# Small loads moved to another queue and the entry of the second block put in another order, in a two-block transformer kernel

## The chip, the cores and the metric

The kernel runs on one core of one Trainium2 chip. The metric is the device time of one execution in microseconds; three timed runs of the kernel before gave a median of 1160.46 us (1156.91 to 1160.65). The core's engines are named as in the profile: PE (TensorE, with PEld for its weight loads), DVE (VectorE), ACT (ScalarE), POOL (GpSimd) and SP (SyncE, which here only issues transfers).

## The reference, cut to what matters

The reference is a network of two blocks on 256 tokens of width 1024, in float32. The first block has two adaptive-norm layers (differential attention with rotary embedding and a context of 256 tokens, then a multi-scale pooling layer), each with a gated feed-forward network; the modulation vectors come from a matrix product with the condition. The second block takes the first one's output:

```
def second_block(x, norm1_g, norm2_g, w_in, qk_norm_g, ...):
    h = _rms(x, norm1_g[layer])
    (a_q, a_k, a_v, i_q, i_k, i_w, b_q, b_kv, b_g, c_qkv, mix_g) = _split_last(h @ w_in[layer], IN_SIZES)
    a_q = _rms(a_q.reshape(bsz, seq, A_HEADS, HEAD_DIM), qk[0])
    a_k = _rms(a_k, qk[1])
    y_a = _dsa_attention(a_q, a_k, a_v, i_q..., i_k, i_w, rel_a) @ w_branch_a[layer]
    ...                     # y_b: compressed, selected and windowed keys; y_c: dilated attention
    x = x + (g[:, :, 0] * y_a + g[:, :, 1] * y_b + g[:, :, 2] * y_c) @ w_out[layer]
    ...                     # second norm and feed-forward network
```

Branch A scores all keys with small index heads (`i_q`, `i_k`, `i_w`), keeps the 64 best keys for each query, and runs softmax attention over them.

## The kernel before, in words

**Matrix products.** Tokens stand in two tiles of 128 (`t` = 0, 1). Each float32 operand is split into a high part (`hi`, a cast on ACT, line 70) and a low part (`lo`, a subtraction on DVE, line 71), and `mm3` (lines 77 to 80) makes three matmuls of each product. Weights come in units of up to 1 MB: `raw_load` (line 54) takes one of four `raw` buffers and starts the load on SP; `wsplit` writes the two parts into a slot, chosen in rotation by `seq["w"]`: slots 0 and 1 are the two buffers of the tag `w`, the others lie in the pools of `extras`.

**Order.** A planner orders each engine's instructions from the order of the program and their dependences. `with behind(i)` orders what is issued inside it behind instruction `i` on that instruction's own engine, without a wait on other engines. A queue runs its instructions strictly in its order, so a waiting instruction holds what stands behind it.

**The first projection.** The weights of the first head group of the first attention are loaded in four quarters by `load_quarter` (keys, queries, values: lines 526 and 498), and the products follow quarter by quarter; `rest(q)` makes the values' and the context keys' part. Behind it seven small loads are issued by ACT (lines 642 to 658): five pieces of `prow` (norm gains and offsets as rows, which line 648 transposes into columns `pcol`), the rotary tables `rope` and the four vectors `lamr` for the differential weight. `rope_T` (lines 676 to 691) rotates keys and queries with four steps on DVE into `r12` and transposes them on PE (line 690).

**The end of the first block.** `o3` is the last output product, with 11 weight units, of which the last three are held and finished per tile and half: `o3.finish(t, n)`. `Norm.pre` adds the residual, `layer_norm` and `rms` normalise the tile (ACT squares with a sum, a square root, a reciprocal, a scaling at line 303), and `to_hT` transposes the scaled tile (line 320) and splits it into `hT` (ACT line 333, DVE lines 336 and 337).

**The entry of the second block.** `KZ`, a zero-padded key buffer, is cleared by POOL (line 936), which then loads `small` (masks, line 946) and `pr2` (positions and gains of queries and keys, lines 951 to 954); `pr2` is transposed at line 956 into `pc2`. `WA` are the bias tables of branch A, loaded by SP. `project(512, 452)` makes keys, values and index heads (`PA`), `project(0, 512, ...)` the queries (`PQ`). For each tile, index queries and keys are copied, transposed (line 1158) and split by `put_q` and `put_k`; `normed_dup_T` norms the keys (line 1042, then the transposes of line 1003). The index scores (line 1169) feed the search for the 64 best (lines 1178 and 1179, on DVE, as a filler of low rank). `gates(0)` makes four gate units with weights as the stationary operand.

`keep_busy(n)` issues `n` matmuls of 128 by 128 ones into a bank that nobody reads.

Of the kernel before, what the change touches and what calls it, by code (L numbers as in the profile page):

```python
# [31 lines left out]
def tile_net(ctx: ExitStack, tc: tile.TileContext, I: dict, out: bass.AP):  # L32
# [49 lines left out]
    def kview(w):  # L82
        return w.rearrange("(k p) n -> p k n", p=128)
# [264 lines left out]
    class Out:  # L348
# [7 lines left out]
        def part(self, u, wh, wl, t, n):  # L356
            mh, ml = self.mov
            tk = slice(t * 128, (t + 1) * 128)
            for k in range(2):
                kk = 2 * u + k  # L360
                mm3(self.P[t][n], mh[:, kk, tk], ml[:, kk, tk], wh[:, k, HALF[n]], wl[:, k, HALF[n]], kk == 0,
                    kk == 2 * self.nu - 1)

        def unit(self, u):
# [105 lines left out]
    with tc.tile_pool(name="at", bufs=1, side="right", reuse_waits="tile") as at:  # L470
# [48 lines left out]
        def load_quarter(q):  # L519

            raws = [raw_load(wv0[:, :, j0 * 128:(j0 + 2) * 128], 8, 256) for j0 in (8 + 2 * q, 2 * q)]
            load_x("x", q)
            rw = wp.tile([128, 2048], F32, tag="raw", name="raw", bufs=4)
            rw = rw[:, :1536].rearrange("p (w k c) -> p w k c", w=3, k=2)
            for i, kind in enumerate((1, 0, 2)):
                sp.dma_start(rw[:, i], wq[:, 2 * q:2 * q + 2, kind * 1024:kind * 1024 + 256])
                if i == 1:
                    load_x("ctx", q)
            return raws, rw
# [41 lines left out]
        class Chunk:  # L571
# [19 lines left out]
            def products(self, ks, lat=True, con=True):  # L591
                wh, wl = self.w
                kw = dict(skip_group_check=True)
                for t in range(2) if lat else ():
                    tk = slice(t * 128, (t + 1) * 128)
                    for k in ks:
                        mm3(self.PL[:, t, :], hT[0][:, k, tk], hT[1][:, k, tk], wh[:, k, :], wl[:, k, :],
                            k == 0 and t == 0, k == 7, **kw)
                if self.kind and con:
                    if self.PC is None:  # L600
                        self.PC = bank().rearrange("p (t c) -> p t c", t=2)
                    for t in range(2):
                        tk = slice(t * 128, (t + 1) * 128)
                        for k in ks:
                            if self.kind == 1:
                                mm3(self.PC[:, t, :], wh[:, k, tk], wl[:, k, tk], hc[0][:, k, :], hc[1][:, k, :],
                                    k == 0 and t == 0, k == 7, **kw)
                            else:
                                mm3(self.PC[:, t, :], hc[0][:, k, tk], hc[1][:, k, tk], wh[:, k, :], wl[:, k, :],
                                    k == 0 and t == 0, k == 7, **kw)  # L610

        ALLK = range(8)
        ck, cq, cv = (Chunk(kind, 0) for kind in (1, 0, 2))
# [2 lines left out]
        def rest(q):  # L616
            ks = range(2 * q, 2 * q + 2)
            cv.products(ks, con=False)
            ck.products(ks, lat=False)

        for q in range(4):
            with behind(*((first_dma.ins,) if not q else ())):
                raws, rw = load_quarter(q)
            mod_quarter(q, raws)
# [11 lines left out]
        oT = [oc.tile([128, 2048], F32R, tag="oT" + i, name="oT", bufs=1).rearrange("p (k c) -> p k c", k=8)  # L636
              for i in ("hi", "lo")]

        with behind(seq["mod"]):
            prow = cp.tile([128, 128], F32, name="prow")  # L640
            gp.memset(prow, 0.0)
            se.dma_start(prow[32:64], I["ln_g"].rearrange("l w (k c) -> (l w k) c", c=128))
            se.dma_start(prow[64:96], I["ln_b"].rearrange("l w (k c) -> (l w k) c", c=128))
            se.dma_start(prow[96:104], rows128(I["norm1_g_2"][0]))
            se.dma_start(prow[104:112], rows128(I["norm2_g_2"][0]))
            se.dma_start(prow[112:113], I["attn_subln_g"])
# [8 lines left out]
            rope = at.tile([128, 2, 2, 2, 64], F32, name="rope")  # L655
            se.dma_start(rope, I["k_rope"].rearrange("(t p) v w c -> p t v w c", p=128))
            lamr = at.tile([128, 256], F32, tag="aT", name="lamr", bufs=5)
            se.dma_start(lamr, I["attn_lambda"].rearrange("a b c -> a (b c)").to_broadcast([128, 256]))
# [231 lines left out]
    with tc.tile_pool(name="hid", bufs=1, side="right", reuse_waits="tile") as hidp:  # L890
# [32 lines left out]
    blk1.close()  # L923
    wi = kview(I["w_in_2"][0])
# [3 lines left out]
    seq["w"] = 2  # L928
    extras.append(ctx.enter_context(tc.tile_pool(name="wz", bufs=1, side="right", reuse_waits="tile")))
    with tc.tile_pool(name="b2", bufs=1, reuse_waits="tile") as b2:  # L930

        KZ = b2.tile([128, 6, 2, 2, 256], F32R, name="KZ")
        for half in range(2):
            gp.memset(KZ[(1 - half) * 64:(2 - half) * 64, :, :, half, :].bitcast(F32), 0.0)

        def vtile():
            return b2.tile([128, 1536], F32, tag="vv", name="vv", bufs=1)
# [4 lines left out]

        small = b2.tile([128, 554], F32, name="small")
        gp.dma_start(small, I["k_small"])
        cmask, eo, bmask = small[:, 0:256], small[:, 256:384], small[:, 384:392]
        nmask = small[:, 392:426].rearrange("p (t n) -> p t n", t=2)
        sel32 = small[0:32, 426:554]
        pr2 = b2.tile([128, 128], F32, tag="t512", name="pr2", bufs=3)  # L950
        gp.memset(pr2, 0.0)
        gp.dma_start(pr2[0:32], I["nsa_cmp_pos_2"][0].rearrange("s (l a) d -> (s l) (a d)", a=2))
        for dup in range(2):
            gp.dma_start(pr2[32:38, dup * 64:(dup + 1) * 64], I["qk_norm_g_2"][0])
        b = tbank()
        pe.transpose(b[:, :128], pr2, ident)
        pc2 = b2.tile([128, 41], F32, name="pc2")
        ve.tensor_copy(pc2[:, 0:38], b[:, 0:38])
        ve.tensor_mul(pc2[:, 38:41], b[:, 32:38:2], pc2[:, 33:38:2])
# [45 lines left out]

        def put(hi, lo, src, scale):

            se.activation(hi, src, AF.Copy, scale=scale)
            ve.scalar_tensor_tensor(lo, src, scale, hi.bitcast(F32), op0=ALU.mult, op1=ALU.subtract)

        def put_k(src, t, d0, scale=1.0):

            n, tk = src.shape[1], slice(t * 128, (t + 1) * 128)
            for half in range(2):
                p = slice(half * 64, (half + 1) * 64)
                put(KZ[p, d0:d0 + n, 0, half, tk], KZ[p, d0:d0 + n, 1, half, tk], src[p],
                    scale if isinstance(scale, float) else scale[p])
# [87 lines left out]
        def gates(br):  # L1105
            g = b2.tile([128, 8, 256], F32, tag="gate", name="gate", bufs=1)
            for u in range(4):
                wh, wl = wunit(wi[:, :, 4572 + br * 1024 + u * 256:4572 + br * 1024 + (u + 1) * 256], 8, 256)
# [78 lines left out]
        for t in range(2):  # L1187
# [270 lines left out]
```

## Time and profile before

| | us |
|---|---|
| median of three timed runs | 1160.46 (1156.91 to 1160.65) |
| the profiled execution, whole | 1157.81 |
| its span, first to last instruction | 1156.0 |
| PE busy | 1129.1 |
| DVE busy | 829.0 |
| ACT busy | 575.8 |

A busy engine is one that executes an instruction; ends of matmuls are modelled. Idle time in front of an instruction is put down to what released it.

### The profile page before, as it was taken

What the parts mean: (1) busy time and instruction counts of PE and PEld (TensorE: products, weight loads), DVE (VectorE), ACT (ScalarE), POOL (GpSimd) and SP (SyncE); (2) the same over time, 40 slices, a digit from 0 to 9 for tenths busy, and PEclk for the clock granted to TensorE, in tenths of its full rate; (3) what the DMA queues carried; (4) which work ended last, traced back from release to release, by engine and by line L of the source; (5) the groups of instructions that cost most, each with busy time, mean ns of one, the idle gap of its engine ahead of it and who ended that gap; (6) DMA issues with size and microseconds to landing.
All of it is one profiled execution on the core that took longest, in us unless ns stands there. A gap on an engine that the chain in (4) does not pass through costs nothing. (4 is left out here: it accounts for less than half of the span.)

```text
span 1156.0 us, 19870 instructions
## 1 busy us (share of the span) xinstructions
PE 1129.1 (98%) x7967; PEld 1035.3 (90%) x7967; DVE 829.0 (72%) x1547; ACT 575.8 (50%) x1017; POOL 83.9 (7%) x154
## 2 busy tenths in 40 slices
PE   8989999999999999999999889999999999999998
PEld 7979988889999877999988779989999989999986
DVE  5677887887887877856654779788788674655541
ACT  5643444576444436654543655455346356545430
POOL 0101110100111111000000020000100000000000
PEclk9999999999999999999999999999999999999999
DMA  9956545648998993867565353660456254664530
GB/s 311 324 174 212 183 155 174 219 146 285 313 317 291 341 353 121 249 217 257 210 222 175 109 180 121 179 200 29 146 160 223 77 178 147 219 199 167 215 113 37
DMA packets 149098, 229.69 MB, mean 199 GB/s; under 512 B 5708, under 2 KB 121051, under 8 KB 149006
## 3 DMA queue, kind: packets, MB, share of 16 engines
q1 hardware_dynamic: 133440, 176.10, 46.6%
q0 software_dynamic: 14672, 50.63, 13.0%
q10 hardware_dynamic: 894, 1.69, 0.5%
q8 instruction: 63, 1.03, 0.4%
q14 instruction: 29, 0.24, 0.1%
HBM read 226.36 MB, written 2.04 MB: 198 GB/s over the span
## 5 line engine op out<-in xcount | busy, mean ns | idle before, releaser
L71 DVE TENSOR_TENSOR wlo<-raw,whi 128x1024 fp32r<-128x1024 f32 (+2 forms) x318 | 372.7, 1193 | 135.2 <-ACT whi L70 133.7
L70 ACT CAST whi<-raw 128x1024 fp32r<-128x1024 f32 (+2 forms) x318 | 316.3, 1028 | 229.6 <-PE mm L80 86.7
L78 PE MATMUL mm<-hTh,whi 128*128 128x256 f32 x1056 | 299.1, 283 | 0.0
L80 PE MATMUL mm<-hTh,wlo 128*128 128x256 f32 x1056 | 298.9, 283 | 0.0
L79 PE MATMUL mm<-hTl,whi 128*128 128x256 f32 x1056 | 298.3, 282 | 0.0
L79 PEld LDWEIGHTS mm<-hTl,whi 128*128 128x128 f32 x1056 | 199.4, 189 | 0.3
L78 PEld LDWEIGHTS mm<-hTh,whi 128*128 128x128 f32 x1056 | 199.3, 189 | 0.3
L80 PEld LDWEIGHTS mm<-hTh,wlo 128*128 128x128 f32 x1056 | 199.3, 189 | 0.1
L78 PE MATMUL mm<-whi,hTh 128*128 128x256 f32 (+4 forms) x592 | 185.5, 314 | 2.3 <-DVE hTh L336 1.8
L80 PE MATMUL mm<-whi,hTl 128*128 128x256 f32 (+4 forms) x592 | 184.8, 313 | 0.4 <-DVE hTl L337 0.4
L79 PE MATMUL mm<-wlo,hTh 128*128 128x256 f32 (+4 forms) x592 | 184.3, 312 | 0.6 <-DVE wlo L71 0.6
L78 PEld LDWEIGHTS mm<-whi,hTh 128*128 128x128 f32 x592 | 112.4, 190 | 9.0 <-DVE hTh L336 2.9
L79 PEld LDWEIGHTS mm<-wlo,hTh 128*128 128x128 f32 x592 | 112.3, 190 | 4.9 <-DVE wlo L71 1.0
L80 PEld LDWEIGHTS mm<-whi,hTl 128*128 128x128 f32 x592 | 111.9, 189 | 5.2 <-DVE hTl L337 1.0
L132 DVE SCALAR_TENSOR_TENSOR acc<-mraw,csil,acc 128x1024 f32<-128x1024 f32 x80 | 102.2, 1280 | 10.0 <-DMA mraw<-in_w_mod_dram 9.6
L78 PE MATMUL mm<-whi,hid 128*128 128x512 f32 x264 | 104.3, 395 | 0.0
L79 PE MATMUL mm<-wlo,hid 128*128 128x512 f32 x264 | 104.2, 395 | 0.0
L80 PE MATMUL mm<-whi,hid 128*128 128x512 f32 x264 | 103.7, 393 | 0.0
L131 POOL DMA_DIRECT2D mraw<-in_w_mod_dram x80 | 42.6, 533 | 367.8 <-DVE acc L132 269.8
L79 PEld LDWEIGHTS mm<-wlo,hid 128*128 128x128 f32 x264 | 49.6, 188 | 11.6 <-issue 1.0
L80 PEld LDWEIGHTS mm<-whi,hid 128*128 128x128 f32 x264 | 49.6, 188 | 11.5 <-issue 0.7
L78 PEld LDWEIGHTS mm<-whi,hid 128*128 128x128 f32 x264 | 49.6, 188 | 11.4 <-issue 0.7
(329 smaller groups left out, 1556.6 us busy)
## 6 DMA issues: line engine op xcount, KB each, us to landing
raw<-in_ffn_w_in_dram SPq DMA_DIRECT2D x44, 1024.0 KB, 7.1
mraw<-in_w_mod_dram POOLq DMA_DIRECT2D x80, 512.0 KB, 5.0
raw<-in_ffn_w_out_dram SPq DMA_DIRECT2D x22, 1024.0 KB, 4.9
raw<-in_w_ffn_in_dram SPq DMA_DIRECT2D x22, 1024.0 KB, 5.2
raw<-in_w_in_dram SPq DMA_DIRECT2D x16, 1024.0 KB, 5.5
raw<-in_w_ffn_out_dram SPq DMA_DIRECT2D x11, 1024.0 KB, 5.0
raw<-in_w_in_dram SPq DMA_DIRECT2D x14, 768.0 KB, 4.4
raw<-in_attn_w_qkv_dram SPq DMA_DIRECT2D x9, 1024.0 KB, 8.4
```

The source lines that it names most:

```text
L70: se.copy(hv[:, sl], raw[:, sl])
L71: seq["sub"] = ve.tensor_sub(lv[:, sl], raw[:, sl], hv[:, sl].bitcast(F32)).ins
L78: pe.matmul(o, lh, rh, start=first, stop=False, **kw)
L79: pe.matmul(o, lh, rl, start=False, stop=False, **kw)
L80: return pe.matmul(o, ll, rh, start=False, stop=last, **kw).ins
L131: gp.dma_start(raw, wv[:, k, g * 1024:(g + 1) * 1024])
L132: ve.scalar_tensor_tensor(acc, raw, csil[:, k, 0:1], acc, op0=ALU.mult, op1=ALU.add)
```

## The change

1. The seven small loads of the first attention (`prow`, `rope`, `lamr`) are issued by SP, directly behind the last load of the last quarter, in place of ACT behind the last modulation. The transpose of `prow` and what follows it are ordered behind the last product of `rest(3)` and the last weight split of the quarters.
2. `pr2` is loaded, transposed and copied into `pc2` ahead of the last output product of the first block, in a buffer of the norm's pool; `pc2` moves to the constant pool.
3. The two weight units of `PA` are loaded and split ahead of the last norm: the first into slot 0, the second into two `raw` buffers. `PA` is made tile by tile, with 14 dummy matmuls behind the first tile.
4. In the last norm `o3.finish(1, 1)` is ordered ahead of the first tile's transposes, with 6 dummy matmuls between them.
5. `small` is loaded ahead of the clearing of `KZ`; `seq["w"]` starts at 0 in the second block; the keys' norm stands ahead of the index heads; the gates' weight casts are ordered behind the last split of the index keys.

The rest are return values that carry these instructions.

```diff
-            se.dma_start(...)                      # seven of them, behind(seq["mod"])
+            if q == 3:
+                with behind(seq["ld"]):
+                    prow = cp.tile([128, 128], F32, name="prow")
+                    gp.memset(prow, 0.0)
+                    sp.dma_start(prow[32:64], I["ln_g"].rearrange("l w (k c) -> (l w k) c", c=128))
...
+                    sp.dma_start(rope, I["k_rope"].rearrange("(t p) v w c -> p t v w c", p=128))
+                    lamr = at.tile([128, 256], F32, tag="aT", name="lamr", bufs=5)
+                    sp.dma_start(lamr, I["attn_lambda"].rearrange("a b c -> a (b c)").to_broadcast([128, 256]))
-        with behind(seq["mod"]):
+        with behind(seq["mod"], seq["rest"], *seq["fill"]):
             pcol_ps = sbank()
             pe.transpose(pcol_ps[:, :128], prow, ident)
...
         f.rest(hT, 1, 3)
+        pr2 = pools["xp"].tile([128, 2, 128], F32, tag="f", name="pr2", bufs=4)[:, 0, :]
+        gp.memset(pr2, 0.0)
+        gp.dma_start(pr2[0:32], I["nsa_cmp_pos_2"][0].rearrange("s (l a) d -> (s l) (a d)", a=2))
...
+        pe.transpose(b[:, :128], pr2, ident)
+        pc2 = cp.tile([128, 41], F32, name="pc2")
...
         o3 = f.out(I["ffn_w_out"][1], 3)
+        wi = kview(I["w_in_2"][0])
+        uA = [raw_load(wi[:, 4 * u:4 * u + 4, 512:964], 4, 452) for u in range(2)]
+        uA[0] = wsplit(uA[0], 4, 452, 0)
+        parts = [wp.tile([128, 2048], F32R, tag="raw", name=nm, bufs=4)[:, :1808].rearrange("p (a b) -> p a b", a=4)
+                 for nm in ("whi", "wlo")]
+        for sl in (slice(0, 2), slice(2, 4)):
+            se.copy(parts[0][:, sl], uA[1][:, sl])
+            ve.tensor_sub(parts[1][:, sl], uA[1][:, sl], parts[0][:, sl].bitcast(F32))
+        uA[1] = parts
...
             n4.rms(t)
-            n4.to_hT(t, hT, N1)
+            if t == 0:
+                P11 = o3.finish(1, 1)
+            with behind(*((keep_busy(6, o3.last),) if t == 0 else ())):
+                n4.to_hT(t, hT, N1)
             if t == 0:
                 with behind(n4.scaled[0]):
-                    n4.pre(1, 1, o3.finish(1, 1), grow)
+                    n4.pre(1, 1, P11, grow)
...
-        PA = project(512, 452)
+        PA = [bank(), bank()]
+        for t in range(2):
+            tk = slice(t * 128, (t + 1) * 128)
+            for k in range(8):
+                wh, wl = uA[k // 4]
+                i = mm3(PA[t][:, :452], hT[0][:, k, tk], hT[1][:, k, tk], wh[:, k % 4, :], wl[:, k % 4, :], k == 0, k == 7)
+            if t == 0:
+                keep_busy(14, i)
...
+        normed_dup_T(PA, 0, 1, 1, GA)
...
-            put_k(bv[:, 2:3], t, 0)
-        normed_dup_T(PA, 0, 1, 1, GA)
+            seq["ix"] = put_k(bv[:, 2:3], t, 0)
...
-        gA_ = gates(0)
+        gA_ = gates(0, *seq["ix"])
```

## Rows read from the trace of the kernel before

**Rows 1.** The page: busy time, share of the span, instructions.

```profile
PE 1129.1 (98%) x7967; PEld 1035.3 (90%) x7967; DVE 829.0 (72%) x1547; ACT 575.8 (50%) x1017; POOL 83.9 (7%) x154
```

**Rows 2.** Waits of PE, whole span: us in total, times, longest us.

```profile
PE tp L956 <- DMA pr<-in_qk_norm_g_dram: 3.1, 1, 3.1
...
PE tp L320 <- ACT z L303: 2.0, 2, 1.1
...
PE tp L1003 <- DVE kn L1042: 1.8, 1, 1.8
...
PE s L648 <- DMA prow<-in_norm_g_dram: 0.7, 1, 0.7
```

**Rows 3.** Timeline of PE, 63 to 72 us: start, duration, instruction, [idle before].

```profile
62.88 0.28 PE L78 MATMUL mm<-whi,hcT 128*128 128x256 f32 x1
...
63.12 0.28 PE L80 MATMUL mm<-whi,hcTl 128*128 128x256 f32 x1
65.94 0.65 PE L690 MATMUL tp<-idsel,r 128*128 128x128 f32 x4 [2.55 <-DVE r L687]
...
66.91 0.41 PE L79 MATMUL mm<-wlo,hcT 128*128 128x256 f32 x1
...
69.89 0.41 PE L78 MATMUL mm<-whi,hTh 128*128 128x256 f32 x1
```

**Rows 4.** Stretches of 10 us: length, busy time of PE, PEld, DVE, ACT, POOL, granted clock, DMA.

```profile
60.00:70.00 10.00, 7.45 (x52) 7.25 (x51) 7.26 (x20) 4.38 (x6) 0.00 (x0) 0.85 0.41 119
...
650.00:660.00 10.00, 8.12 (x33) 6.64 (x34) 6.38 (x22) 7.13 (x23) 0.00 (x0) 0.83 0.71 210
```

**Rows 5.** Timeline of ACT and its queue, then of DVE, 36 to 80 us.

```profile
53.21 0.32 ACTq L642 DMA_DIRECT2D prow<-in_ln_g_dram  x1
...
55.73 0.48 ACTq L658 DMA_DIRECT2D lamr<-in_attn_lambda_dram  x1
...
57.93 1.05 ACT L70 CAST whi<-raw 128x1024 fp32r<-128x1024 f32 x1
...
61.78 0.69 DVE L684 TENSOR_TENSOR r<-mm,rope 128x512 f32<-128x512 f32 x1 [1.63 <-DMA rope<-in_k_rope_dram]
```

**Rows 6.** Timeline of the queue of SP around 38 us.

```profile
38.15 0.43 SPq L526 DMA_DIRECT2D raw<-in_attn_w_qkv_dram  x1
...
38.69 0.56 SPq L54 DMA_DIRECT2D raw<-in_attn_w_qkv_dram  x1
```

**Rows 7.** Timeline of PE, 16 to 18 us: dummy matmuls.

```profile
16.35 1.60 PE L103 MATMUL s<-ones 128*128 128x128 f32 x12
```

**Rows 8.** Timeline of PE, 636 to 702 us.

```profile
647.31 0.39 PE L80 MATMUL mm<-whi,hid 128*128 128x512 f32 x1
...
650.40 0.61 PE L78 MATMUL mm<-whi,hTh 128*128 128x452 f32 x1 [0.52 <-DVE hTh L336]
...
656.77 0.36 PE L80 MATMUL mm<-whi,hTl 128*128 128x452 f32 x1
...
659.89 0.47 PE L78 MATMUL mm<-whi,hTh 128*128 128x452 f32 x1 [0.43 <-DVE hTh L336]
...
664.95 0.40 PE L78 MATMUL mm<-whi,hTh 128*128 128x512 f32 x1
...
684.42 0.36 PE L78 MATMUL mm<-hTh,whi 128*128 128x256 f32 x1
```

**Rows 9.** Timeline of ACT, then of POOL, 630 to 702 us.

```profile
645.67 1.78 ACT L70 CAST whi<-raw 128x904 fp32r<-128x904 f32 x2
...
662.48 5.39 POOL L936 MEMSET KZ<- 64x3072 f32 x2 [81.70 <-ACT whi L70]
```

**Rows 10.** Stretches of 20 us, columns as in rows 4.

```profile
660.00:680.00 20.00, 16.85 (x81) 13.96 (x82) 14.10 (x29) 12.13 (x28) 9.89 (x12) 1.00 0.65 195
680.00:700.00 20.00, 18.09 (x140) 16.82 (x139) 19.80 (x70) 13.05 (x21) 0.00 (x0) 1.00 0.36 130
```

**Rows 11.** The page: transfers by line, KB each, median us from issue to landing.

```profile
raw<-in_w_in_dram SPq DMA_DIRECT2D x16, 1024.0 KB, 5.5
```

More of the change, by code (lines that the diff above doesn't have):

```diff
@@ L360, in part @@
                 kk = 2 * u + k
-                mm3(self.P[t][n], mh[:, kk, tk], ml[:, kk, tk], wh[:, k, HALF[n]], wl[:, k, HALF[n]], kk == 0,
+                self.last = mm3(self.P[t][n], mh[:, kk, tk], ml[:, kk, tk], wh[:, k, HALF[n]], wl[:, k, HALF[n]], kk == 0,
                     kk == 2 * self.nu - 1)
@@ L525, in load_quarter @@
             for i, kind in enumerate((1, 0, 2)):
-                sp.dma_start(rw[:, i], wq[:, 2 * q:2 * q + 2, kind * 1024:kind * 1024 + 256])
+                seq["ld"] = sp.dma_start(rw[:, i], wq[:, 2 * q:2 * q + 2, kind * 1024:kind * 1024 + 256]).ins
                 if i == 1:
@@ L605, in products @@
                             if self.kind == 1:
-                                mm3(self.PC[:, t, :], wh[:, k, tk], wl[:, k, tk], hc[0][:, k, :], hc[1][:, k, :],
+                                i = mm3(self.PC[:, t, :], wh[:, k, tk], wl[:, k, tk], hc[0][:, k, :], hc[1][:, k, :],
                                     k == 0 and t == 0, k == 7, **kw)
                             else:
-                                mm3(self.PC[:, t, :], hc[0][:, k, tk], hc[1][:, k, tk], wh[:, k, :], wl[:, k, :],
-                                    k == 0 and t == 0, k == 7, **kw)
+                                i = mm3(self.PC[:, t, :], hc[0][:, k, tk], hc[1][:, k, tk], wh[:, k, :], wl[:, k, :],
+                                        k == 0 and t == 0, k == 7, **kw)
+                    return i
         ALLK = range(8)
@@ L618, in rest @@
             cv.products(ks, con=False)
-            ck.products(ks, lat=False)
+            seq["rest"] = ck.products(ks, lat=False)
         for q in range(4):
@@ L623, in tile_net @@
                 raws, rw = load_quarter(q)
+            if q == 3:
[3 more added lines that the diff above has]
+                    sp.dma_start(prow[32:64], I["ln_g"].rearrange("l w (k c) -> (l w k) c", c=128))
+                    sp.dma_start(prow[64:96], I["ln_b"].rearrange("l w (k c) -> (l w k) c", c=128))
+                    sp.dma_start(prow[96:104], rows128(I["norm1_g_2"][0]))
+                    sp.dma_start(prow[104:112], rows128(I["norm2_g_2"][0]))
+                    sp.dma_start(prow[112:113], I["attn_subln_g"])
+                    rope = at.tile([128, 2, 2, 2, 64], F32, name="rope")
+                    sp.dma_start(rope, I["k_rope"].rearrange("(t p) v w c -> p t v w c", p=128))
+                    lamr = at.tile([128, 256], F32, tag="aT", name="lamr", bufs=5)
+                    sp.dma_start(lamr, I["attn_lambda"].rearrange("a b c -> a (b c)").to_broadcast([128, 256]))
             mod_quarter(q, raws)
@@ L637, in tile_net @@
               for i in ("hi", "lo")]
-        with behind(seq["mod"]):
[L640 to L646, printed above, removed]
+        with behind(seq["mod"], seq["rest"], *seq["fill"]):
             pcol_ps = sbank()
@@ L654, in tile_net @@
             N1, N2 = pcol[:, 96:104], pcol[:, 104:112]
[L655 to L658, printed above, removed]
             lsum = at.tile([128, 4], F32, name="lsum")
@@ L898, in tile_net @@
         f.rest(hT, 1, 3)
-        o3 = f.out(I["ffn_w_out"][1], 3)
+        pr2 = pools["xp"].tile([128, 2, 128], F32, tag="f", name="pr2", bufs=4)[:, 0, :]
+        gp.memset(pr2, 0.0)
+        gp.dma_start(pr2[0:32], I["nsa_cmp_pos_2"][0].rearrange("s (l a) d -> (s l) (a d)", a=2))
+        for dup in range(2):
+            gp.dma_start(pr2[32:38, dup * 64:(dup + 1) * 64], I["qk_norm_g_2"][0])
+        b = tbank()
+        pe.transpose(b[:, :128], pr2, ident)
+        pc2 = cp.tile([128, 41], F32, name="pc2")
+        ve.tensor_copy(pc2[:, 0:38], b[:, 0:38])
+        ve.tensor_mul(pc2[:, 38:41], b[:, 32:38:2], pc2[:, 33:38:2])
+        o3 = f.out(I["ffn_w_out"][1], 3)
+        wi = kview(I["w_in_2"][0])
[7 more added lines that the diff above has]
+        uA[1] = parts
         mod_until("g2_1")
@@ L927, in tile_net @@
     yacc = yo.tile([128, 8, 256], F32, name="yacc")
-    seq["w"] = 2
+    seq["w"] = 0
     extras.append(ctx.enter_context(tc.tile_pool(name="wz", bufs=1, side="right", reuse_waits="tile")))
     with tc.tile_pool(name="b2", bufs=1, reuse_waits="tile") as b2:
-        KZ = b2.tile([128, 6, 2, 2, 256], F32R, name="KZ")
-        for half in range(2):
-            gp.memset(KZ[(1 - half) * 64:(2 - half) * 64, :, :, half, :].bitcast(F32), 0.0)
         def vtile():
@@ L946, in tile_net @@
         gp.dma_start(small, I["k_small"])
+        KZ = b2.tile([128, 6, 2, 2, 256], F32R, name="KZ")
+        for half in range(2):
+            gp.memset(KZ[(1 - half) * 64:(2 - half) * 64, :, :, half, :].bitcast(F32), 0.0)
         cmask, eo, bmask = small[:, 0:256], small[:, 256:384], small[:, 384:392]
@@ L949, in tile_net @@
         sel32 = small[0:32, 426:554]
[L950 to L959, printed above, removed]
         GA, GB, GC = pc2[:, 38:39], pc2[:, 39:40], pc2[:, 40:41]
@@ L1006, in put @@
         def put(hi, lo, src, scale):
-            se.activation(hi, src, AF.Copy, scale=scale)
-            ve.scalar_tensor_tensor(lo, src, scale, hi.bitcast(F32), op0=ALU.mult, op1=ALU.subtract)
+            i = se.activation(hi, src, AF.Copy, scale=scale)
+            return i.ins, ve.scalar_tensor_tensor(lo, src, scale, hi.bitcast(F32), op0=ALU.mult, op1=ALU.subtract).ins
         def put_k(src, t, d0, scale=1.0):
@@ L1015, in put_k @@
                 p = slice(half * 64, (half + 1) * 64)
-                put(KZ[p, d0:d0 + n, 0, half, tk], KZ[p, d0:d0 + n, 1, half, tk], src[p],
-                    scale if isinstance(scale, float) else scale[p])
+                i = put(KZ[p, d0:d0 + n, 0, half, tk], KZ[p, d0:d0 + n, 1, half, tk], src[p],
+                        scale if isinstance(scale, float) else scale[p])
+            return i
         def put_q(dst, src, t, d0, scale=1.0):
@@ L1103, in split_oT, with gates @@
             ve.tensor_sub(oTl[:, :nb, tk], bv, oTh[:, :nb, tk].bitcast(F32))
-        def gates(br):
+        def gates(br, *after):
             g = b2.tile([128, 8, 256], F32, tag="gate", name="gate", bufs=1)
             for u in range(4):
-                wh, wl = wunit(wi[:, :, 4572 + br * 1024 + u * 256:4572 + br * 1024 + (u + 1) * 256], 8, 256)
+                with behind(*after):
+                    wh, wl = wunit(wi[:, :, 4572 + br * 1024 + u * 256:4572 + br * 1024 + (u + 1) * 256], 8, 256)
                 G = bank().rearrange("p (a b) -> p a b", a=2)
```

1 line of the change is left out of this document (removed).

## The prediction

> **What bounds the kernel now.** I read the share of each engine first: TensorE (PE) is busy 98% of the span [rows 1], so time can only be won where PE stands still or runs on a slow clock. Next the waits of PE over the whole span: five entries carry most of its idle time, and nearly all of them lie in two places, the end of the first projection (58 to 70 us) and the entry of the second block (647 to 685 us) [rows 2, 3]. Elsewhere PE waits little, so what is won in one place should not be waited for again later, as long as VectorE (DVE) and the weight loads keep up. The granted clock by stretches of 10 us is well below 1.00 in three only; two of them lie in these places [rows 4].
>
> **First place: the small loads.** Seven loads are issued by ScalarE (ACT) from 53.21 to 56.21 us, 3.0 us in all [rows 5]. `prow` is late for the transpose on line 648, which costs PE 0.7 us [rows 2]. `rope` lands only at 61.78 us, so the four DVE steps of `rope_T` start there, and the transposes behind them keep PE waiting for 2.55 us, from 63.25 to 65.94 [rows 3, 5]. Then the clock falls: from 66.91 to 69.89 us lie 14 steps of 0.213 us, where the same matmul took 0.12 us before (62.88 to 63.12, two steps) [rows 3], the granted clock of 60 to 70 us being 0.85 [rows 4]. Some 15 matmuls lose 0.093 us each: 1.4 us.
>
> After the change SyncE issues these loads directly behind the last load of the last quarter, issued at 38.15 us [rows 6]. I cost the issue at the same 3.0 us: they are out at 41.7. Today `rope` lands 8.6 us behind the first of these issues (53.21 to 61.78); even counted from the last issue that makes 50.3, some eight microseconds before the first use at about 58.8. `rope_T` for the keys can then start as soon as its sums are done, which PE writes before line 648's transpose, and is off PE's path. Gain: 0.7 + 2.55 + 1.4 = 4.65, 4.7 us. Bounds: at least 3.2, the two stalls alone, if the clock falls anyway; no more than 4.7, because PE has no other wait here.
> What does it delay? SyncE's next instruction, a 1 MB weight load for the second head group, goes out at 38.69 us today and is first cast at 57.93 [rows 5, 6]. Three microseconds later it still has more than fifteen in hand: it costs nothing, and the later loads on SyncE wait for free buffers, not for SyncE. If that cover were gone, it would cost up to 3.0 us. ACT is spared 3.0 us of issuing, after which it waits for PE today: that brings nothing either.
> The rows say that the date of issue decides, not the queue. The Trainium skill, "DMA: Bandwidth & Descriptors", section "Issuing engines are not separate DMA queues", speaks against expecting anything of a change of queue: transfers started by any engine share the same 16 DMA engines and interleave. By that rule the move is worth only what the earlier issue is worth, and its price is SyncE's issue time. That agrees with the sum above, which takes no bandwidth gain.
>
> **Second place, the norm in front of the second block.** Today ACT casts the second half of the first weights (2 casts, 1.78 us) at 645.67 us, in the middle of the first tile's norm [rows 9]; the square root that the norm needs next stands behind the second of them, some 0.9 us. PE waits twice for the scaled tiles, 2.0 us together [rows 2]. The change makes both casts before the norm (where ACT has little to do), orders the last sums of the output matmul ahead of the first tile's transposes, adds 6 dummy matmuls between them and 14 behind the first tile's product. A dummy costs 0.133 us (12 took 1.60) [rows 7]: 0.8 and 1.9 us, 2.7 in all.
> Who ends last here? The first tile's 24 matmuls run from 650.40 to 656.97 at half clock for most of it (the granted clock is 0.83), then PE waits for the second tile, whose 24 start at 659.89 and take 5.06 us [rows 4, 8]. So the 1.5 us that the slow clock costs (6.57 against 5.06) are hidden behind the second tile's norm, and so are the dummies: the first tile would end at about 655.0 at full clock, the 14 dummies at 656.9, and the second tile's transposes are due at about 657.8 (659.89 less 1.7 for themselves and the first split, less 0.4). What counts is how much earlier the second norm is done. Its multiply-add on DVE loses the weights' subtraction in front of it (about as long as one such cast), but its squares still queue on ACT behind the eight scalings of the first tile, which start only some 0.3 us earlier because 0.8 us of dummies stand where PE waits about 1.0 us today (half of the 2.0). I take 0.4 us of gain; from below minus 0.8 (dummies in the way of the transposes, if the first tile runs at half clock), from above 1.3.
>
> **Third, the entry itself.** From the second tile's start to the first gate matmul PE takes 24.53 us (659.89 to 684.42) [rows 8]. In these lie two waits: 3.1 us for the load of `pr2` and 1.8 us for the normed keys `kn` [rows 2]. `pr2` is issued only when GpSimd has cleared `KZ` (from 662.48, 5.39 us) [rows 9]. After the change it is loaded and transposed before the first block's last output product, well before its use, so 3.1 us go. The keys' norm moves ahead of the index heads, so its chain of small DVE steps starts when `PA` is done (664.95 today, where the first query matmul of 512 columns starts) and not behind the wait for `pr2`; beside it PE has 48 query matmuls, each no shorter than the 0.211 us of one of 452 columns (5.06 by 24), some 10 us: 1.8 us go. What is left is 24.53 - 4.9 = 19.6 us of work. Moving `small` ahead of the clearing costs GpSimd one issue (0.5 us), nobody waits for it. Keeping the first tile's and second tile's product apart costs nothing; PE runs them in that order today.
> Against this: DVE is busy 14.10 of 20 us in 660 to 680, but 19.80 of 20 in 680 to 700 [rows 10]. When PE comes 5 us earlier, DVE must do 5 us more before 680. It has 5.9 us idle there, so it fits, barely; I charge 0.5 us for new short waits. From above the charge is the whole 4.9.
> The cast of the gates' weights now queues behind the index keys. Its first load goes out ahead of the norm today; after the change two of the four raw buffers hold weights until the second tile's product ends, so it goes out at about 664.5 and lands 5.5 us later [rows 11], at 670; cast and subtraction take some 3 us more (two casts of 1.05 us [rows 5] and a subtraction behind the second). PE needs it at 659.5 + 19.6 = 679.1. Six microseconds of cover: nothing.
>
> **The sum.** 4.7 + 0.4 + 3.1 + 1.8 - 0.5 = 9.5 us. The profiled execution took 1157.81 us (span 1156.0 and 1.8 around it): 1148.3. It lies 2.65 under the median of the three timed runs, 1160.46, which spread from 1156.91 to 1160.65; from the median the sum gives 1151.0. I forecast 1149.5, between the two, a gain of 0.9%.
>
> **The rivals.**
> *DVE takes over at the entry.* For: the 19.80 of 20 us above. Against: it is partly filler (the search for the 64 best is issued as filler), and DVE's idle time lies just where the work moves. Then the 4.9 us come back as waits on DVE, and 4.7 + 0.4 remain: 1152.7 from the profile, 1155.4 from the median; about 1154.
> *The small loads don't help.* The order only puts them behind the last quarter; if the planner issues weight loads ahead of them, or if PE finds the next late thing (the query's rope or the second group's weights), the first place gives 0 to 1 us: 1153 to 1155. Against: three weight loads could pass and they would still land in time.
> *The clock falls again.* With the dummies done at 656.9 and the second tile at 659.5, PE does nothing but transposes for 2.6 us. Today two such pauses of 2.9 us lie ten microseconds apart: in the first (647.54 to 650.40) the clock fell, in the second (656.97 to 659.89) it did not, the stretch 660 to 680 stands at 1.00 [rows 4, 8, 10]. If it falls in front of the second tile, that tile's matmuls take 6.57 instead of 5.06, and nothing hides it: plus 1.5 us, 1151. The Trainium skill, "TensorE: Matmul & The Clock Gate", section "Part 4: PE-mode transpose", says that transposes do not count as PE activity in the way matmuls do; by that rule the transposes do not shorten this pause. That the clock fell at 650 after a pause holding eight transposes agrees.
> *Slower.* The gates' weights come late: their buffers free at 664.5, four 1 MB loads then go out at once beside the bias loads. It decides when the first gate unit is ready later than 679.1 + 9.5 = 688.6, which is a landing 21 us after the issue where 5.5 is usual. Each microsecond beyond is lost on PE; at 27 us the kernel takes about 1164. Little speaks for it.
>
> **How the numbers follow.** The forecast 0.60 (1146 to 1152.5 with the bounds of the norm and of the two references); the clock 0.12 (1151); DVE 0.13 (1152.5 to 1157); the small loads 0.07 (1153 to 1157); slower 0.05; two rivals together 0.03 (no change). A measurement of this kernel tells 0.3%, 3.5 us, from nothing: under 1157.0 is faster. Of the DVE and small-load cases, a third sits at that line. Faster 0.82, same 0.12, slower 0.06. The range is 1145.5 to 1157.5: the low end is all waits and the norm's best bound gone, the high end the DVE rival at its worst from the median.
>
> **What the profile after would show.** Right: no wait on line 648's transpose nor for `r`; the clock at 1.00 from 60 to 80 us; PE's waits for `pr2` and `kn` gone; the first gate matmul 19.6 to 20.1 us after the second tile's first matmul; dummies in stretches that were idle. Wrong: new waits of PE for a DVE step between 664 and 720 us (DVE has become the bound); PE waiting for the gates' weights (the buffers); the second tile's transposes directly behind a dummy with no idle time (the dummies cost); a granted clock under 1.00 in the entry.

## The result and the profile after

The changed kernel takes 1150.35 us (median of 4 runs, 1150.09 to 1150.97), the kernel before on the same chip 1158.68 (4 runs): a ratio of 0.993, 95% interval 0.991 to 0.995. So it is faster, by 0.7%, and the interval is clear of 1. The forecast was 1149.5. The profiled execution took 1150.09 us (span 1148.3) against 1157.81: 7.7 us less, where the sum said 9.5.

PE's four largest waits over the whole span (us in total, times, longest). The entries for `pr2`, `r` and line 648 of [rows 2, 3] have no successor; `kn`'s is down from 1.8 to 1.0:
```profile
PE mm L78 <- DVE hTh L336: 2.1, 4, 1.3
PE tp L1019 <- DVE qn L1046: 1.5, 5, 0.4
PE tp L841 <- ACT z L281: 1.3, 1, 1.3
PE tp L1019 <- DVE kn L1059: 1.0, 1, 1.0
```
Stretches of 10 us (length, busy time of PE, PEld, DVE, ACT and POOL with its count, granted clock, DMA share, GB/s): both slow stretches of [rows 4] run at the full clock now.
```profile
60.00:70.00 10.00, 9.75 (x76) 8.76 (x76) 9.49 (x12) 8.45 (x14) 0.00 (x0) 1.00 0.92 307
650.00:660.00 10.00, 10.00 (x66) 9.42 (x65) 6.98 (x15) 8.06 (x19) 4.28 (x3) 1.00 0.15 33
```
SyncE's issues behind the last quarter's loads (start, length), which answer to [rows 6]:
```profile
38.47 0.43 SPq L526 DMA_DIRECT2D raw<-in_attn_w_qkv_dram  x1
39.01 0.41 SPq L630 DMA_DIRECT2D prow<-in_ln_g_dram  x1
41.17 0.33 SPq L631 DMA_DIRECT2D prow<-in_ln_b_dram  x1
41.91 0.28 SPq L632 DMA_DIRECT2D prow<-in_norm_g_dram  x1
...
44.22 0.47 SPq L638 DMA_DIRECT2D lamr<-in_attn_lambda_dram  x1
44.88 1.08 SPq L54 DMA_DIRECT2D raw<-in_attn_w_qkv_dram  x2
```
And SyncE's waits in 40 to 44 us:
```profile
SPq L631 <- DMA raw<-in_w_mod_dram: 1.7, 1, 1.7
SPq L634 <- DMA raw<-in_attn_w_qkv_dram: 0.5, 1, 0.5
SPq L633 <- DMA raw<-in_attn_w_qkv_dram: 0.5, 1, 0.5
SPq L632 <- DMA x<-in_x_dram: 0.4, 1, 0.4
```
PE from the end of the output product to the second tile, which answers to [rows 8] (a row of line 103 is the dummies):
```profile
641.69 0.40 PE L80 MATMUL mm<-whi,hid 128*128 128x512 f32 x1
641.93 1.50 PE L103 MATMUL s<-ones 128*128 128x128 f32 x12
643.26 1.04 PE L320 MATMUL tp<-idsel,z 128*128 128x128 f32 x8
645.63 0.48 PE L78 MATMUL mm<-whi,hTh 128*128 128x452 f32 x1 [1.33 <-DVE hTh L336]
...
650.76 1.28 PE L103 MATMUL s<-ones 128*128 128x128 f32 x10
651.91 0.66 PE L320 MATMUL tp<-idsel,z 128*128 128x128 f32 x4
652.40 0.39 PE L103 MATMUL s<-ones 128*128 128x128 f32 x2
652.63 0.60 PE L320 MATMUL tp<-idsel,z 128*128 128x128 f32 x4
653.07 1.95 PE L103 MATMUL s<-ones 128*128 128x128 f32 x16
654.77 0.46 PE L78 MATMUL mm<-whi,hTh 128*128 128x452 f32 x1
...
676.09 0.28 PE L78 MATMUL mm<-hTh,whi 128*128 128x256 f32 x1
...
962.11 0.65 PE L320 MATMUL tp<-idsel,z 128*128 128x128 f32 x4
```
Where the 7.7 us came from. The end of the output product moved from 647.70 to 642.09: 5.6 us. From there to the last transposes in front of the second block's feed-forward (969.35 before, 962.11 after) PE took 321.65 us before and 320.02 now: the whole entry gave 1.6 us. I call this the *entry stretch* below, since it leaves out what happens in the first place and in the feed-forwards. The last 0.5 us lie in the second block's feed-forward, which the change doesn't touch (last section).

The 5.6 us hold some chance. In the eight kernels that differ only behind this point (the changed one and experiments 3, 5, 6, 8, 9, 10 and 12) the product ends anywhere from 641.69 to 646.09, so the first place is better read from the medians of experiment 1. The entry stretch is steadier: in experiments 2 and 7, which leave the entry alone, it takes 319.83 and 320.00 us, against 320.02.

### The profile page after: what moved, and what is told of

It is laid out like the page before. It is cut to its first block, busy times and chain, and to the rows that moved or that the text cites. A ratio compares the mean times of both kernels' runs of the same rounds, so it can differ in the third digit from the quotient of the medians.

```text
span 1148.3 us, 19946 instructions
## 1 busy us (share of the span) xinstructions
PE 1131.3 (99%) x8007; PEld 1040.0 (91%) x8007; DVE 832.0 (72%) x1547; ACT 575.5 (50%) x1017; POOL 84.1 (7%) x154
## 3 DMA queue, kind: packets, MB, share of 16 engines
q8 instruction: 63, 1.03, 0.4%
## 4 chain that ended last, share of the span: by engine, by line
PE 90%; DVE 6%; ACT 2%; issue 1%; DMA 1%; SPq 0%; DVEq 0%; ACTq 0%
PE mm L80 25%; PE mm L78 25%; PE mm L79 25%; PE tp L1095 2%; PE s L1067 2%; DVE wlo L71 2%; PE s L710 2%; PE tp L734 1%; PE tp L1091 1%; PE s L138 1%; DMA raw<-in_w_mod_dram 1%; PE tp L721 1%; PE mm L886 1%; PE s L145 1%; PE s L541 1%
```

## The experiments

All ratios are to the kernel before, run on the same chip. The entry stretch is read from PE's rows of each run's profile.

| kernel | ratio, 95% interval | entry stretch, us |
|---|---|---|
| before | 1 | 321.65 |
| changed | 0.993, 0.991 to 0.995 | 320.02 |
| 1 small loads only | 0.9949, 0.993 to 0.9968 | 323.19 |
| 2 loads on ScalarE, early | 0.9983, 0.997 to 0.9995 | 319.83 |
| 3 no dummies | 0.9924, 0.9901 to 0.9947 | 318.07 |
| 4 `pr2` late | 0.9985, 0.9969 to 1.0 | 326.53 |
| 5 without the 6 | 0.9918, 0.99 to 0.9935 | 317.48 |
| 6 without the 14 | 0.9916, 0.99 to 0.9932 | 318.55 |
| 7 loads on ScalarE, tied | 0.9954, 0.994 to 0.9968 | 320.00 |
| 8 index heads first | 0.9926, 0.9909 to 0.9942 | 318.16 |
| 9 as 5 and 8 together | 0.9914, 0.9892 to 0.9935 | 316.27 |
| 10 as 9, gates untied | 0.9913, 0.9892 to 0.9933 | 316.22 |
| 11 small loads and `pr2` only | 0.9931, 0.9911 to 0.9952 | 319.29 |
| 12 as 9, no dummies | 0.9908, 0.9885 to 0.9932 | 317.16 |

**1. The small loads alone**: the kernel before with only the seven loads moved, and the order of the products and sums around them that the change has.
```diff
-                    se.dma_start(prow[32:64], ...)      # and six more, behind the last products
+                    sp.dma_start(prow[32:64], ...)      # and six more, behind seq["ld"]
```


> The kernel before with the first part alone: the seven small loads issued by SyncE behind the last quarter's, and the transpose of `prow` behind the last product of `rest(3)`. Theory (the early date of these loads is worth the two stalls and the slow clock behind them): PE's waits on `prow` and on `r` are gone, the granted clock is 1.00 from 60 to 80 us, and the kernel takes 4.7 to 5.6 us less than the one before, about 1153.5. Rival (the first place gives little by itself, most of the gain is at the entry of the second block): less than 2 us, 1157 or more. The entry should look as before: waits of about 3.1 us on `pr2` and 1.8 us on `kn`.


1152.58 us against 1157.49: 4.9 us by the medians, 5.9 by the ratio, about the expected size. The entry stretch grew by 1.5 us, with this stretch of 10 us at the lower clock, where before stands at 1.00 [rows 10]:
```profile
670.00:680.00 10.00, 8.41 (x35) 6.58 (x35) 7.42 (x33) 4.85 (x14) 0.00 (x0) 0.83 0.54 154
```

**2. The same loads on ScalarE, early**: the tie is to the third quarter's cast, not to the last quarter's load.
```diff
-                with behind(seq["ld"]):
-                    sp.dma_start(...)   # seven
+                with behind(seq["fill"][0]):
+                    se.dma_start(...)   # seven
```


> The changed kernel with the seven small loads issued by ScalarE again, but behind its last weight split of the third quarter (about 36 us, some 15 us earlier than in the kernel before). Theory (the date of issue decides, not the queue): within 1 us of the changed kernel, 1149.5 to 1151.5, no wait of PE on `prow` or `r`. Rival (the queue matters, because ScalarE's issuing holds its casts, or because the transfers then share the engines with the last quarter's loads): 1 to 3 us of new waits of PE between 36 and 60 us, 1151.5 to 1154.


1156.23 us, above the rival's 1154 too: all of the first place's gain is gone (by the ratio 2.0 us are left, about what the entry gives; the output product ends at 649.11, 1.4 us later than in the kernel before). The waits of PE and of SyncE name it:
```profile
PE tp L563 <- DMA xin<-in_ctx_dram: 3.2, 2, 2.5
...
SPq L526 <- DMA prow<-in_ln_g_dram: 6.2, 1, 6.2
```
SyncE held back a load of the last quarter for 6.2 us, until `prow` had landed; the context load behind it came late, PE waited 3.2 us for it, and the clock fell in 50 to 60 us (0.83). The date is not what differs: ScalarE issued `prow` here at 38.53 us, SyncE in the changed kernel at 39.01. The row of `prow`'s issue, and that of the load which waited for it:
```profile
38.53 0.32 ACTq L630 DMA_DIRECT2D prow<-in_ln_g_dram  x1
41.94 0.88 SPq L526 DMA_DIRECT2D raw<-in_attn_w_qkv_dram  x2
```
SyncE had stood there since 35.70 us, so for 2.8 us it waited for a load that ScalarE had yet to issue. What the program puts ahead of the last quarter's loads delays them, even when another engine issues it. My theory, that only the date of issue decides, fell.

**3. No dummies**: both calls of `keep_busy` in the entry left out (they compute nothing that is used).
```diff
-            with behind(*((keep_busy(6, o3.last),) if t == 0 else ())):
-                n4.to_hT(t, hT, N1)
+            n4.to_hT(t, hT, N1)
 ...
-            if t == 0:
-                keep_busy(14, i)
```


> The changed kernel without both groups of dummy matmuls (6 in front of the first tile's transposes, 14 behind the first tile's product). Theory (they stand on the path: in the trace of the changed kernel the 6 take 1.5 us in front of transposes whose data is ready, and 8 of the 14 run between the second tile's first split and its first matmul, 1.2 us after that split is done): the second tile starts 1.0 to 2.3 us earlier, 1148 to 1149.3, with the granted clock at 1.00. Rival (they hold the clock): the clock falls near the first or second tile; if in front of the second, its 24 matmuls take 6.6 instead of 5.0 us, 1149.5 to 1151.


1149.83 us, no slower than the changed kernel; the entry stretch is 1.95 us shorter. The second tile starts 1.47 us earlier, as the theory said, although the clock falls in 650 to 660 us (0.83), as the rival said. So the dummies together cost more than the clock they hold.

**4. `pr2` late again**: its load, transpose and copies moved back behind the clearing of `KZ`.
```diff
-        pr2 = pools["xp"].tile(...); gp.memset(pr2, 0.0); gp.dma_start(pr2[0:32], ...)   # ahead of f.out
+        pr2 = b2.tile(...); gp.memset(pr2, 0.0); gp.dma_start(pr2[0:32], ...)            # behind the clearing of KZ
```


> The changed kernel with `pr2` loaded and transposed at its old place, behind the clearing of `KZ`. Theory (the early `pr2` is worth PE's 3.1 us wait of the kernel before): a wait of PE for `pr2` of 2 to 4 us comes back, 1152.5 to 1154.5. Rival (with the keys' norm moved ahead, the wait for `pr2` would lie beside the 1.0 us that PE waits for `kn` anyway, so that little is lost): under 1.5 us, 1150.4 to 1151.9.


1156.74 us, beyond both expectations, and an entry stretch 6.5 us longer than the changed kernel's: more than twice what the wait itself measures. PE's row of the wait:
```profile
670.61 0.30 PE L969 MATMUL tp<-idsel,pr 128*128 128x128 f32 x1 [2.66 <-DMA pr<-in_qk_norm_g_dram]
```
And the stretch that it ends in:
```profile
670.00:680.00 10.00, 9.39 (x40) 7.22 (x41) 4.89 (x14) 6.15 (x19) 0.00 (x0) 0.83 0.67 187
```
Behind the 2.66 us matmuls run at the lower clock, and VectorE is busy 4.89 of 10 us there, where it had 9.05 in the changed kernel (whose output product ended 2.2 us sooner). It must do that work later, and from 680 to 690 us it is busy 10.00 of 10.

**5 and 6. One group of dummies at a time**, each without one of the two calls of experiment 3.

> The changed kernel (1150.35 us) without the 6 dummy pairs in front of the second block's first tile; the 14 stay. Theory (the 6 stand on the path): with them the first tile's first matmul comes 3.54 us behind the output product's end, in the run without any dummies 1.73 us, so 1.8 us come off: about 1148.5 us, and that tile still runs at the full clock. Rival (they keep the clock): the granted clock falls in the first tile, whose first nine matmuls then take 0.38 instead of 0.205 us apart, 1.6 us: 1150.2 us, no gain.

> The changed kernel without the 14 dummy pairs in front of the second tile; the 6 stay. Theory (they hold the clock and cost little): the second tile starts 0.3 us sooner, and its first nine matmuls run at the lower clock, 0.38 instead of 0.205 us apart, 1.6 us: 1151.7 us, with a granted clock near 0.83 in 650 to 660 us. Rival (they only stand in the way; behind the transposes 1.2 us of them are left): about 1149.2 us.

Without the 6 the entry stretch is 2.5 us shorter, where the theory said 1.8, and the clock holds, as it said; the time, 1149.4 us, is a ratio of 0.9918 against the changed kernel's 0.993, with intervals that overlap. PE's rows:
```profile
644.44 0.39 PE L80 MATMUL mm<-whi,hid 128*128 128x512 f32 x1
644.78 1.27 PE L320 MATMUL tp<-idsel,z 128*128 128x128 f32 x8
646.56 0.48 PE L78 MATMUL mm<-whi,hTh 128*128 128x452 f32 x1 [0.51 <-DVE hTh L336]
...
651.67 2.84 PE L103 MATMUL s<-ones 128*128 128x128 f32 x24
654.35 1.26 PE L320 MATMUL tp<-idsel,z 128*128 128x128 f32 x8
655.45 0.61 PE L103 MATMUL s<-ones 128*128 128x128 f32 x4
656.04 0.47 PE L78 MATMUL mm<-whi,hTh 128*128 128x452 f32 x1
```
The first tile starts 1.73 us behind the product's end (644.83 to 646.56), with the 6 it was 3.54 (642.09 to 645.63). And 24 of the 28 records of the 14 now lie in PE's wait for the second tile, ahead of its transposes, where with the 6 only ten did and sixteen lay behind.

Without the 14 the time, 1149.49 us, is near the rival's 1149.2, but neither mechanism held as it stood. The clock did fall (0.83 in 650 to 660), and the second tile's 24 matmuls took 6.67 us instead of 5.01; but the tile started 1.16 us sooner, and the 1.03 us wait for `kn` is gone, which took back most of the 1.66. The entry stretch is 1.5 us shorter.

**7. The loads on ScalarE behind the last quarter's loads.**
```diff
-                    sp.dma_start(prow[32:64], ...)   # seven, behind seq["ld"]
+                    se.dma_start(prow[32:64], ...)
```


> The changed kernel with the seven small loads still behind the last quarter's loads, but issued by ScalarE. Theory (what counts is that they stand behind the last quarter's loads in the order of issue; the engine that issues them does not): the context load goes out by 38 us, no wait for xin, 1150.4 us within 0.6. Rival (ScalarE's queue costs): 2.7 us of issue stand between ScalarE's casts and modulations at 39 to 45 us, and with no slack there the first projection ends 2 to 3 us later: 1152.5 to 1153.5 us.


1153.68 us; but it tested something else. The tie puts an order on the program, not on another engine's queue, and ScalarE had nothing ahead of them to wait for. ScalarE's issues:
```profile
1.19 0.42 ACTq L630 DMA_DIRECT2D prow<-in_ln_g_dram  x1
...
3.93 0.63 ACTq L638 DMA_DIRECT2D lamr<-in_attn_lambda_dram  x1
```
At 1 to 5 us they stand beside the very first weights, which everything waits for. The first cast of these weights starts at 8.15 us instead of 7.48, SyncE's next issues wait 1.1 us for `prow` and 0.8 us for `rope` to land, and `prow`'s transpose comes at 61.3 us instead of 59.2. The clock falls in 10 to 20 us (0.83), but this can't be put down to the early loads: it falls there in experiments 2, 4, 5, 9, 10 and 11 too (0.83 to 0.87), where ScalarE issues none of the seven so soon. In those six the first product (line 78) starts at 18.97 to 19.33 us, here at 20.72, in the changed kernel, at the full clock, at 18.52. So 1.4 to 1.8 of the 2.2 us belong to the loads, and the rest may be chance.

By the ratios this kernel loses 2.8 us against the changed one, and experiment 2 loses 6.1: a place too far ahead can cost as much as being late. Whether ScalarE would do as well as SyncE, with the loads behind the last quarter's in its own queue too, was not tried.

**8. The old order**: the keys' norm behind the index heads again.
```diff
-        normed_dup_T(PA, 0, 1, 1, GA)
         for t in range(2):
             ...
+        normed_dup_T(PA, 0, 1, 1, GA)
```


> The changed kernel with the keys' normalisation put behind the index heads' work again. Theory (the reorder is worth what the wait lost): the wait for kn, now 1.0 us, goes back to 1.8 us or more, and VectorE's charge of 0.5 us comes off again: 1150.7 to 1151.2 us. Rival (the reorder is the entry's main gain, since the gate's first matmul comes 2.7 us sooner relative to the output product): 1152.5 to 1153.0 us. Third (it is worth nothing, the gain is pr2's alone): 1150.4 us.


By the entry stretch all three theories missed: it is 1.9 us *shorter* with the old order, and the wait for `kn` is 0.2 us, not 1.8. The time (ratio 0.9926) can't tell it from the changed kernel. The stretch 660 to 670 of the changed kernel:
```profile
660.00:670.00 10.00, 8.77 (x40) 6.22 (x39) 7.45 (x29) 4.62 (x17) 3.84 (x6) 1.00 1.06 315
```
The same stretch of this one, and the one from 680:
```profile
660.00:670.00 10.00, 9.64 (x46) 6.88 (x45) 9.32 (x39) 7.08 (x19) 3.88 (x6) 1.00 1.07 325
680.00:690.00 10.00, 9.45 (x79) 9.03 (x78) 9.97 (x40) 5.70 (x7) 0.00 (x0) 1.00 0.54 163
```
VectorE (the third of the busy times) does 1.87 us less in the changed kernel, about what that kernel loses. From 680 to 690 us it is full in either (9.97 of 10). The chain of steps that makes `kn` stands at the start of this; VectorE's rows of the changed kernel:
```profile
660.85 0.93 DVE L1012 TENSOR_SCALAR ss<-ss 128x2 f32<-128x2 f32 x1
661.81 0.17 DVE L234 TENSOR_SCALAR rs<-ss 128x2 int32<-128x2 int32 x1
662.02 0.16 DVE L236 TENSOR_TENSOR rs<-rs 128x2 f32<-128x2 f32 x1
...
664.07 0.62 DVE L1059 TENSOR_TENSOR kn<-mm,rs 128x64 f32<-128x64 f32 x4
```
Each small step starts 0.2 us behind the one before, and nothing else runs on VectorE between them. ScalarE stands idle meanwhile: its copies of the values and the index heads start only when `kn` is nearly done. And PE has its transposes of `kn` behind only 15 of the 48 query matmuls:
```profile
664.46 0.48 ACT L1177 COPY vA<-mm 128x64 f32<-128x64 f32 x2 [4.25 <-DVE kn L1059]
664.48 0.33 PE L1019 MATMUL tp<-idsel,kn 128*128 128x128 f32 x1 [1.03 <-DVE kn L1059]
```
Between 664.7 and 669 us VectorE then waits 1.7 us in all for what ScalarE makes of the transposed keys and index heads. In the old order ScalarE makes these copies from 656.55 us on, and the index heads' steps on VectorE lie between those of the chain. Why ScalarE's copy, which doesn't read `kn`, waits for it, the trace doesn't show.

**9 and 10. Both taken out, then the gates' tie too**: the edits of 5 and 8 together; then also `gates(0)` in place of `gates(0, *seq["ix"])`.

> The changed kernel without the 6 dummy pairs and with the keys' normalisation behind the index heads again; the 14 stay. From the output product's end to the second block's feed-forward transposes the changed kernel takes 320.0 us, the run without the 6 takes 317.5 and the run with the old order 318.2. Theory (the two costs are separate): both come off, 315.6 us for that stretch, and the time is about 1146.0 us. Rival (both end in the same wait on VectorE, so that one hides the other): 317 to 317.5 us, and 1147.5 to 1148.0 us.

> As the kernel before it in this call, and the first gate's weights no longer tied behind the index keys. Theory (the tie only sets an order that the engines follow anyway): the same time within 0.6 us. Rival (the tie keeps the gate's casts and subtractions out of the keys' chain on VectorE): 1 to 2 us slower, with a longer wait for kn.

9 is 3.75 us shorter in the entry stretch than the changed kernel, of 4.4 if the two costs were separate: the theory, less an overlap of 0.65. (So the reorder costs 1.9 us beside the 6 and 1.2 us without them, 317.48 less 316.27.) Its 1148.55 us are 0.86% under the kernel before; by the ratios that is 1.8 us under the changed kernel, but the two intervals overlap. In 10 the tie makes no difference (0.05 us).

**11. The small loads and `pr2`, nothing else.**
```diff
+        pr2 = pools["xp"].tile(...)   # load, transpose and copies ahead of f.out, as in the change
         o3 = f.out(I["ffn_w_out"][1], 3)
 ...
-        pr2 = b2.tile(...)            # behind small
```


> The kernel before with the small loads moved (1152.6 us) and pr2 loaded, transposed and copied early; the rest of the entry as before. Theory (pr2's wait of 2.0 to 3.1 us is on the path, with the slower clock behind it): 2 to 3.5 us off, 1149.1 to 1150.6 us, which is all that the whole entry gives, since its reorder and its dummies take back what its other edits bring. Rival (the wait only moves to kn, whose 1.8 us grow to 4): 1152.0 us or more.


1149.94 us, ratio 0.9931: as fast as the whole change. `pr2` takes 3.9 us off the entry stretch of experiment 1 (2.4 off that of the kernel before, which has no slow clock in 670 to 680 us), and `kn`'s wait is gone with it.

**12. As 9, without the 14 dummies.**

> The fastest kernel so far (without the 6, keys' normalisation behind the index heads, 316.27 us from the output product's end to the feed-forward transposes) without the 14 dummy pairs too. Theory (the 14 hold the clock, and in this order nothing behind swallows it): 1.6 us more, 317.9 us for that stretch and the lower clock in the second tile, about 1150.0 us. Rival (the normalised queries on VectorE end last whatever PE's clock is): 316.3 to 316.7 us, 1148.5 us. If the theory holds, the preloaded weights and the order of the sums are worth 319.3 less 317.9, 1.4 us; by the rival 3.0 us.

The entry stretch is 0.9 us longer than with them, between the two theories, at the lower clock (650 to 660, 0.83). The median, 1147.63, can't be told from 9's.

## Why the prediction was right, and where its terms were not

The direction and the size hold: 8.3 us between the medians, 7.7 between the profiled executions, forecast 1149.5 against 1150.35. That the time is met within 1 us is in part luck. The terms of the second block (0.4 + 3.1 + 1.8 - 0.5) make 4.8 us, and the entry stretch gave 1.6, or 3.2 counted from experiment 1's; PE's lead in front of it, 5.6 us, lies above the 4.7, and the forecast had been set 1.2 us above the sum's 1148.3.

One reading at its start was off: the "five entries" of PE's waits sum to 11.2 us, of 26.9 us in which PE isn't busy, so they are the largest entries, but not most of its idle time.

*Small loads, 4.7 us: right.* Alone they give 4.9 us (experiment 1); in the profile after, PE goes from 0.4 us behind the kernel before (at 50 us) to 4.8 ahead (at 190 us), 5.2 in all. Both waits and the slow clock of [rows 3] are gone. The step inside it that was wrong is SyncE's issue, "3.0 us, out at 41.7": it took 5.7, to 44.69. The issues themselves are no longer than thought (2.4 us); 3.1 us are waits for older loads to land. Line 631 waits for the load issued at 34.07, eight issues earlier, and 632 to 634 likewise. The cover of more than fifteen microseconds held, so it cost nothing.
"The date of issue decides, not the queue" was too simple. In experiment 2 the date was the same and the place in the program's order was not: 6.1 us lost. In experiment 7 the loads went out at 1 to 5 us: 2.8 us lost. The rule cited from the Trainium skill, "DMA: Bandwidth & Descriptors", "Issuing engines are not separate DMA queues", speaks of sharing between transfers; experiment 7 agrees with it in part (with ScalarE's loads beside them the first weights are cast at 8.15 us, not 7.48). Experiment 2's price is another: a SyncE issue that waits 6.2 us for ScalarE's load to land.

*The norm, 0.4 us gained: it lost.* The second tile starts 12.68 us behind the output product's end, before it was 12.19; without the 6 it is 11.21 (experiment 5), and without any dummies too (3): the rest of the change brings about 1.0 us there, and the dummies take 1.5. The step that failed is the size of a dummy: 12 records in 1.60 us [rows 7] are six dummies, each recorded as two matmuls (the 6 leave 12 records, the 14 leave 28), so one takes 0.267 us, not 0.133. The 20 take 5.1 us (1.50 + 1.28 + 0.39 + 1.95 in the rows after) and were costed at 2.7, hidden. The 6 stand on the path, and sixteen records of the 14 lie between the transposes and the second tile, which was split before they ended. "The second tile's transposes directly behind a dummy" was named as the sign of that.

*`pr2`, 3.1 us: right in kind; the size depends on what stands beside it.* It is 2.4 us against the stretch of the kernel before, 3.9 against experiment 1's (both by experiment 11), and 6.5 when it is undone in the changed kernel (4), where the stall drags the clock and VectorE's work behind it.

*`kn`, 1.8 us: wrong.* 0.8 of the wait went, and the reorder that was to remove it costs 1.9 us (experiment 8) or 1.2 (9 against 5). With `pr2` early the old order has only 0.2 us of wait there. Two steps failed. The overlap with the 48 query matmuls: PE's transposes of `kn` stand behind 15 of them, 3.5 us, while the chain takes 4.1 us from VectorE's sum of the second tile's squares (660.60) to its end. And the chain's earlier start was taken for a gain, without counting what ScalarE and VectorE do meanwhile. The charge of 0.5 us for VectorE was too small: this is the rival "DVE takes over" in part, but by idling ahead of its full stretch. From the second tile to the first gate matmul PE took 21.32 us, not 19.6 to 20.1; in the old order 20.44 (8), and 19.71 without the 6 as well (9).

*The clock* did not fall in the entry, as forecast, because of the 14. Without them it falls (3, 6, 12); the second tile's matmuls then take 1.66 us more in experiment 6, near the rival's 1.5, and the entry stretch grows by 0.9 us in experiment 12. *The gates' weights* were never late: PE has no wait for them.

In sum the reorder, the dummies, the weights' casts and the ties cancel: experiment 11 has the whole gain without them. What the casts ahead of the norm and the order of the last sums are worth by themselves was not run alone; by experiment 12 against 11 they are worth 2.1 us of the entry stretch, together with `PA` made tile by tile, the move of `small` and the gates' tie.

## What to carry to other kernels

Count a filler by its records against its instructions, and ask what becomes ready while it runs: a dummy that fills a wait is free, one ahead of transposes that are ready, or behind the last ones, is on the path. When an engine is full in the stretch behind, what counts is that it never idles in front of it: a chain of tiny dependent steps belongs between other work, not ahead of it. A load wanted soon goes directly behind the last load that is wanted sooner, in the order of the program too; further ahead it delays the other.

## What was not expected of the hardware

In the 256-column matmuls of the feed-forwards, at a granted clock of 1.00, the same instruction stream runs at one of a few steady paces in different executions: 117.3 ns a matmul in the second layer of the changed kernel (1040 to 1060 us), 118.3 before, 118.7 in experiment 8 (means over 20 us of PE's rows). From the last transposes above to the end that makes 186.2, 186.65 and 187.3 us, and all 14 profiles lie within 0.1 us of one of these three. So one profile against another carries up to 1.1 us in this feed-forward that no edit made, which is why experiments of 1 to 2 us are read from the entry stretch here. What sets the pace was not found.

In the profile after, SyncE's issues of the small loads (lines 631 to 634) each waited for the landing of the load eight issues before; and not of SyncE's alone: in experiment 2 a SyncE load stood 6.2 us for one that ScalarE issued, and in the kernel before one stood 8.2 us for ScalarE's `prow`. So where a load stands in the order of both engines' loads counts, and not only when it is issued.
